# A transformer block in emulated fp32: seven-product steps for the second FFN's first matrix, transposes issued by ScalarE, and a norm spread over one more tile

## The chip, the core and the metric

The kernel runs on one core of a Trainium2 chip. The time is that of the device for one call, in microseconds (us); lower is better. The core's engines work side by side and each takes its instructions in order: PE (TensorE) multiplies, DVE (VectorE) and ACT (ScalarE) work on elements, POOL (GpSimd) does little here, and SP (SyncE) issues transfers. DMA engines carry the transfers out.

## The reference, cut to what matters

One block for a sequence of 256 rows and a width of 2048: two feed-forward networks (FFN) around a mixer of attention and convolution. Each part works on a normed and modulated x, and adds to x.

```python
def modulate(h, shift, scale):
    return h * (1 + scale[:, None, :]) + shift[:, None, :]

def swiglu(h, w_gu, w_down):
    gu = jnp.einsum('bsd,df->bsf', h, w_gu)        # 2048 -> 2 * 5632
    g, u = jnp.split(gu, 2, axis=-1)
    return jnp.einsum('bsf,fd->bsd', jax.nn.silu(g) * u, w_down)

    ada = jnp.einsum('bd,de->be', c_act, w_ada[l]) + b_ada[l]
    sh1, sc1, g1, shm, scm, gm, sh2, sc2, g2 = jnp.split(ada, N_MOD, axis=-1)
    h = modulate(rms_norm(x, ffn1_norm[l]), sh1, sc1)
    x = x + FFN_RESIDUAL_WEIGHT * g1[:, None, :] * swiglu(h, ffn1_w_gu[l], ffn1_w_down[l])
    ...                                             # the mixer, in the same form
    h = modulate(rms_norm(x, ffn2_norm[l]), sh2, sc2)
    x = x + FFN_RESIDUAL_WEIGHT * g2[:, None, :] * swiglu(h, ffn2_w_gu[l], ffn2_w_down[l])
```

All weights are fp32 and are read once from DRAM.

## The kernel before

**Products.** An fp32 product is made of three products of a shorter kind (fp32r): both factors are split into a high and a low part, and high x high, high x low and low x high are summed in a PSUM bank (`mm3`, L329, L333, L334). ACT makes the high part of a weight tile (a cast, L305), DVE the low part (a subtraction, L307). A weight arrives as a `raw` tile of 128 x 2048 (1 MB, four buffers), which `w_tile` splits into two `whi` and two `wlo` tiles of 128 x 1024 (four buffers each).

**An FFN.** The 2 x 5632 gate and up columns are cut into 22 chunks of 256 + 256 columns, and the 2048 rows that are summed over into four K blocks of 512 (`pc` 0 to 3). The 256 rows of x are two tiles of 128 (`t`). A chunk and a K block make one step: four column blocks of 128 rows of K, two row tiles, three products, 24 matmuls of 128 x 512. First, K block 0 of all chunks is done and copied to SBUF (`stage_a`, L666), since the norm of the later K blocks is not there yet; then the chunks follow one by one with K blocks 1 to 3. `finish` adds the kept part (L830), applies silu (L831) and multiplies (L832). The result has to be turned for the down projection: in the second FFN, ACT rearranges it to 16-bit planes (L836), SP issues a DMA transpose (L842), ACT joins the planes again (L845), and ACT and DVE split the turned tile (L350, L351).

**Down.** `down_strassen` takes the 2048 output columns in two halves. For 7 of 22 chunks (`SEVEN`) the step of 2 x 2 blocks is done in seven block products instead of eight (a form of Strassen's), at the price of sums of weight blocks on DVE (`split`, L512, L513, and L547 to L550).

**The norm.** `Norm.piece` scales four column blocks of x; one tile later (`after_tiles(1, ...)`, a list that each tile of products counts down in `tick`) `complete` transposes them on PE (L394), modulates them on DVE (L449) and ACT (L452), and splits them (L453, L454). The modulation is computed on the way: `ada` reads 142 pieces of 1 MB of `w_ada` and multiplies them with c on DVE (L193), spread over the program by `ada_share`.

**The order.** The code is a sequence of calls; a scheduler that knows the tiles' buffers and dependences puts the instructions of each engine in an order at build time. Each engine then runs its own list, with semaphores between them. All transfers are issued by SP.

## Time and profile before

| | before |
|---|---|
| median of 3 runs | 1826.58 us (1826.22 to 1826.65) |
| profiled execution | 1831.11 us, span 1829.3 us |
| PE, DVE, ACT busy | 1802.8, 1519.9, 1008.3 us |
| DMA | 501.68 MB, mean 274 GB/s |

A span goes from the first to the last instruction of the profiled execution. Rows of the profile name the line of the kernel, the engine, the operation, and what is written from what (`wlo<-raw,whi`), by the names in the program; a group has its count, the busy time in us, the mean of one in ns, and the idle time before its instructions with what ended it.

### The profile page before, as it was taken

What the parts mean: (1) busy time and instruction counts of PE and PEld (TensorE: products, weight loads), DVE (VectorE), ACT (ScalarE), POOL (GpSimd) and SP (SyncE); (2) the same over time, 40 slices, a digit from 0 to 9 for tenths busy, and PEclk for the clock granted to TensorE, in tenths of its full rate; (3) what the DMA queues carried; (4) which work ended last, traced back from release to release, by engine and by line L of the source; (5) the groups of instructions that cost most, each with busy time, mean ns of one, the idle gap of its engine ahead of it and who ended that gap; (6) DMA issues with size and microseconds to landing.
All of it is one profiled execution on the core that took longest, in us unless ns stands there. A gap on an engine that the chain in (4) does not pass through costs nothing.

```text
span 1829.3 us, 21896 instructions
## 1 busy us (share of the span) xinstructions
PE 1802.8 (99%) x8117; PEld 1484.0 (81%) x8117; DVE 1519.9 (83%) x2018; ACT 1008.3 (55%) x1521; POOL 28.3 (2%) x29
## 2 busy tenths in 40 slices
PE   7999999999999999999999999999999999999998
PEld 5788888888888887788888787888888888878887
DVE  6889869999898787898999778878887765699877
ACT  6553444444444344566798655664665565555453
POOL 0000000000000000000110100000000000000000
PEclk9999999999999999999999999999999999999999
DMA  9987978888889998775444466889899877655552
GB/s 373 349 307 297 347 274 310 327 314 337 337 330 350 355 343 327 290 261 206 176 147 162 160 254 241 328 337 346 262 313 298 302 242 222 203 207 210 204 214 109
DMA packets 95962, 501.68 MB, mean 274 GB/s; under 512 B 31424, under 2 KB 31856, under 8 KB 38384
## 3 DMA queue, kind: packets, MB, share of 16 engines
q1 hardware_dynamic: 95856, 500.30, 74.4%
q8 instruction: 63, 1.03, 0.2%
q14 instruction: 43, 0.35, 0.1%
HBM read 492.37 MB, written 2.12 MB: 270 GB/s over the span
## 4 chain that ended last, share of the span: by engine, by line
PE 85%; DVE 6%; DMA 4%; ACT 3%; issue 2%; POOL 0%; POOLq 0%; DVEq 0%; SPq 0%; ACTq 0%
PE acc L333 27%; PE acc L334 27%; PE acc L329 27%; DVE wlo L307 2%; DMA tmp<-tmp 1%; DMA xall<-in_x_dram 1%; PE tp L333 1%; PE tp L334 1%; DMA raw<-in_w_ada_dram 1%; PE tp L329 1%; ACT whi L305 1%; PE acc L1137 1%; DVE raw L193 1%; DVE wlo L513 1%; DVE blk L1029 1%
## 5 line engine op out<-in xcount | busy, mean ns | idle before, releaser
L333 PE MATMUL acc<-wlo,blk 128*128 128x512 f32 x2340 | 913.7, 390 | 6.9 <-DVE wlo L307 6.9
L329 PE MATMUL acc<-whi,blk 128*128 128x512 f32 x2343 | 911.4, 392 | 1.9 <-ACT blk L403 1.4
L334 PE MATMUL acc<-whi,blk 128*128 128x512 f32 x2340 | 912.3, 390 | 0.1
L305 ACT CAST whi<-raw 128x1024 fp32r<-128x1024 f32 (+1 forms) x581 | 597.3, 1044 | 473.3 <-PE acc L334 333.9
L307 DVE TENSOR_TENSOR wlo<-raw,whi 128x1024 fp32r<-128x1024 f32 (+1 forms) x581 | 691.1, 1210 | 177.7 <-ACT whi L305 176.6
L333 PEld LDWEIGHTS acc<-wlo,blk 128*128 128x128 f32 x2340 | 439.6, 188 | 103.1 <-DVE wlo L307 12.9
L329 PEld LDWEIGHTS acc<-whi,blk 128*128 128x128 f32 x2343 | 439.9, 188 | 93.4 <-ACT blk L403 1.8
L334 PEld LDWEIGHTS acc<-whi,blk 128*128 128x128 f32 x2340 | 439.3, 188 | 91.9 <-DVE blk L405 0.7
L193 DVE CUSTOM_DVE_ANT_0 raw<-raw,c_bc 128x2048 f32<-128x2048 f32 x142 | 324.2, 2285 | 10.3 <-DMA raw<-in_w_ada_dram 10.3
L512 ACT CAST whi<-raw 128x1024 fp32r<-128x1024 f32 (+1 forms) x56 | 53.0, 947 | 68.4 <-PE tp L334 31.9
L513 DVE TENSOR_TENSOR wlo<-raw,whi 128x1024 fp32r<-128x1024 f32 (+1 forms) x56 | 60.8, 1087 | 19.1 <-ACT whi L512 18.9
L666 ACT COPY blk<-acc 128x512 f32<-128x512 f32 x72 | 42.0, 590 | 62.9 <-PE acc L334 60.2
L1029 DVE SCALAR_TENSOR_TENSOR blk<-blk,cst,blk 128x245 f32<-128x245 f32 (+21 forms) x176 | 70.4, 457 | 0.6 <-ACT blk L1027 0.5
L845 ACT COPY tmp<-tmp 128x1024 uint16<-128x1024 uint16 x22 | 29.8, 1355 | 51.2 <-DMA tmp<-tmp 51.2
L830 DVE TENSOR_TENSOR blk<-acc,blk 128x512 f32<-128x512 f32 x88 | 56.6, 682 | 0.0
L831 ACT ACTIVATE blk<-blk 128x256 f32<-128x256 f32 x88 | 33.7, 413 | 20.5 <-DVE blk L830 20.4
L329 PE MATMUL acc<-blk,blk 128*128 128x512 f32 x104 | 41.3, 401 | 1.2 <-ACT blk L321 1.2
L333 PE MATMUL acc<-blk,blk 128*128 128x512 f32 x100 | 39.1, 391 | 0.6 <-DVE blk L307 0.6
L334 PE MATMUL acc<-blk,blk 128*128 128x512 f32 x100 | 39.0, 392 | 0.0
L351 DVE TENSOR_TENSOR blk<-tmp,blk 128x512 fp32r<-128x512 f32 x22 | 15.1, 688 | 26.0 <-ACT blk L350 26.0
L832 DVE TENSOR_TENSOR blk<-blk 128x256 f32<-128x256 f32 x88 | 33.8, 417 | 0.4 <-ACT blk L831 0.4
L836 ACT COPY tmp<-blk 128x1024 uint16<-128x1024 uint16 x22 | 22.9, 1042 | 14.2 <-DVE blk L832 14.1
(227 smaller groups left out, 1058.7 us busy)
## 6 DMA issues: line engine op xcount, KB each, us to landing
raw<-in_w_gu_dram SPq DMA_DIRECT2D x161, 1024.0 KB, 6.0
raw<-in_w_ada_dram SPq DMA_DIRECT2D x142, 1024.0 KB, 6.3
raw<-in_w_dn_dram SPq DMA_DIRECT2D x88, 1024.0 KB, 5.4
raw<-in_w_in_dram SPq DMA_DIRECT2D x40, 1024.0 KB, 4.8
raw<-in_w_out_dram SPq DMA_DIRECT2D x16, 1024.0 KB, 4.8
raw<-in_w_gu_dram SPq DMA_DIRECT2D x8, 768.0 KB, 6.5
blk<-in_w_gu_dram SPq DMA_DIRECT2D x10, 512.0 KB, 13.5
blk<-gate_line SPq DMA_DIRECT2D x6, 512.0 KB, 4.8
```

Of the source, the lines that this page charges most:

```text
L193: nc.vector.tensor_tensor_reduce(out=raw, in0=raw, in1=c_bc, scale=1.0, scalar=0.0, op0=ALU.mult, op1=ALU.add, accum_out=ada_cols[g][:, j ...
L305: nc.scalar.copy(out=hi[:, :m, :], in_=rw)
L307: nc.vector.tensor_sub(out=lo[:, :m, :], in0=rw, in1=hi[:, :m, :].bitcast(F32))
L329: nc.tensor.matmul(acc, ah, wh, start=start, stop=False)
L333: nc.tensor.matmul(acc, ah, wl, start=False, stop=False)
L334: return nc.tensor.matmul(acc, al, wh, start=False, stop=stop)
L512: nc.scalar.copy(out=hi[:, :n, :], in_=src)
L513: nc.vector.tensor_sub(out=lo[:, :n, :], in0=src, in1=hi[:, :n, :].bitcast(F32))
L666: last_part[0] = nc.scalar.copy(out=parts[c][:, t, :], in_=accs[t])
L830: nc.vector.tensor_add(out=p[:, t, :], in0=accs[t], in1=p[:, t, :])
L832: nc.vector.tensor_mul(out=p[:, t, 256:], in0=p[:, t, :256], in1=p[:, t, 256:])
L1029: nc.vector.scalar_tensor_tensor(out=y[:, d:], in0=u, scalar=w, in1=y[:, d:], op0=ALU.mult, op1=ALU.add)
```

## The change

It has several parts.

1. **Second FFN, gate and up.** Two neighbouring chunks make a pair; seven pairs (`PAIRS_2`) do K block 3 with seven block products (`pair_first`), 42 matmuls instead of 48. The sums of x blocks are made once (`pair_sums`, as `sums_of` does for down), those of weights for each pair: four subtractions of 128 x 1024 on DVE, seven splits instead of four. ACT copies a bank (`kept`, L710) before PE adds the next product to the same bank; the copies are used in place of the parts that K block 0 left before. The pair's other K blocks follow in the same banks.
2. **Its order.** `AHEAD_2` names how many K blocks of chunks 0 to 13 come first, `REST_2` the order of the chunks and pairs after that.
3. **x** lies in four tiles of the `blk` pool instead of one of its own, loaded in halves; in the second FFN it is written to DRAM (`spill`) and read again at chunk 16 of the down projection (`fetch`).
4. **Transposes by DMA** are issued by ACT (L959), and the join (L970) is called two tiles later.
5. **The norm** takes a tile for its transposes (`turn`, L414) and completes one tile later (modulation L476 and L479, cast L480, low part L481). From the mixer on, modulation is formed for four columns at once and the bias is added for eight.
6. `KEPT` (the sums that the second half of down takes over from the first) is 7 instead of 6, and `ada` is spread a little differently.

```diff
-KEPT = 6
+KEPT = 7
 CROSSBAR = {0: False, 96: True}
+AHEAD_2 = (1,) * 6 + (2,) * 4 + (3,) * 4
+REST_2 = (6, 10, 14, 7, 0, 11, 16, 8, 2, 12, 18, 9, 4, 20, 13)
+PAIRS_2 = (0, 2, 4, 14, 16, 18, 20)
+ROOM_2 = (2, 2, 2, 1, 0, 0, 0)
...
-            after_tiles(1, lambda: self.complete(kb, t))
+            after_tiles(1, lambda: self.turn(kb, t))
+        def turn(self, kb, t):
+            if (kb, t) in self.open:
+                self.turned[kb, t] = self.transposed(self.open.pop((kb, t)))
+                after_tiles(1, lambda: self.complete(kb, t))
 
         def complete(self, kb, t):
-            if (kb, t) not in self.open:
+            if (kb, t) in self.open:
+                self.turned[kb, t] = self.transposed(self.open.pop((kb, t)))
+            if (kb, t) not in self.turned:
                 return
-            tp, hf = self.transposed(self.open.pop((kb, t)))
+            tp, hf = self.turned.pop((kb, t))
...
+    def pair_first(w_gu, c, pc, act, sums, banks, room):
+        raws = []
+        for n in range(2):
+            raw = rawp.tile([P, 4, 512], F32, tag="raw", name=nm("raw"))
+            w_dma[0] = nc.sync.dma_start(out=raw, in_=w_gu[c + n, pc].rearrange("p (k n) -> p k n", k=4))
+            raws += [raw[:, 0:2, :], raw[:, 2:4, :]]
+        b11, b21, b12, b22 = raws
+        c11, c21, c12, c22 = banks
+        def split(src, own=False):
+            hi = blk([P, 2, 512], F32R) if own else whp.tile([P, 2, 512], F32R, tag="whi", name=nm("whi"))
+            lo = blk([P, 2, 512], F32R) if own else wlp.tile([P, 2, 512], F32R, tag="wlo", name=nm("wlo"))
+            nc.scalar.copy(out=hi, in_=src)
+            nc.vector.tensor_sub(out=lo, in0=src, in1=hi.bitcast(F32))
+            return hi, lo
+        def times(acc, a, w, start=False):
+            for j in range(2):
+                mm3(acc, a(j), (w[0][:, j, :], w[1][:, j, :]), start and j == 0, j == 1, more=not start)
+        def kept(acc):
+            u = tmp([P, 512])
+            nc.scalar.copy(out=u, in_=acc)
+            return u
+        k0 = 4 * pc
+        t2 = blk([P, 2, 512])
+        nc.vector.tensor_sub(out=b12, in0=b12, in1=b11)
+        nc.vector.tensor_sub(out=t2, in0=b22, in1=b12)
+        times(c22, lambda j: act(k0 + j, 0), split(b11, room > 0), True)
+        u11 = kept(c22)
+        nc.vector.tensor_sub(out=b11, in0=t2, in1=b11)
+        times(c12, lambda j: sums[j][0], split(b12, room > 1), True)
+        u22 = kept(c12)
+        times(c22, lambda j: sums[j][1], split(t2))
+        u12 = kept(c22)
+        nc.vector.tensor_sub(out=t2, in0=b21, in1=t2)
+        times(c21, lambda j: act(k0 + 2 + j, 1), split(t2), True)
+        times(c11, lambda j: act(k0 + 2 + j, 0), split(b21), True)
+        times(c22, lambda j: sums[j][2], split(b11))
+        u21 = kept(c22)
+        times(c12, lambda j: sums[j][3], split(b22))
+        tick()
+        tick()
+        return [u11, u21, u12, u22]
+    xd = dramp.tile([P, NT, 2, 1024], F32, name="x_kept")
+    def spill(i):
+        if i < 2 * NT:
+            nc.sync.dma_start(out=xd[:, i // 2, i % 2], in_=xb[i // 2][i % 2])
+    def fetch(h):
+        for t in range(NT):
+            xb[t][h] = blk([P, 1024])
+            nc.sync.dma_start(out=xb[t][h], in_=xd[:, t, h])
...
-            for c in range(3, NCH):
-                w = w_tile(w_gu[c, 0])
-                stage_a(c, w, [acc_tile() for _ in range(NT)], (0, 1))
-                ada_a_share(4)
-                pieces()
+            for c, n in enumerate(AHEAD_2):
+                start_of[c] = n
+                if c < 3:
+                    continue
+                accs = [acc_tile() for _ in range(NT)]
+                for pc in range(n):
+                    ada_until(base + 8 * pc + 8)
+                    pieces(last_part[0] if ada_next[0] >= base + 32 else None)
+                    w = w_tile(w_gu[c, pc])
+                    mm_tile(accs, w, act, 4 * pc, pc == 0, pc == n - 1)
+                    ada_a_share(4)
+                    pieces(last_part[0] if ada_next[0] >= base + 32 else None)
+                parts[c] = blk([P, NT, 512])
+                for t in range(NT):
+                    last_part[0] = nc.scalar.copy(out=parts[c][:, t, :], in_=accs[t])
+                spill(c - 6 if c >= 6 else 9)
...
-        def finish(c, accs):
-            p = parts[c]
+        def finish(c, accs, us=None):
+            p = parts[c] or blk([P, NT, 512])
+            m = tmp([P, NT, 256]) if CROSSBAR[base] else p[:, :, 256:]
             for t in range(NT):
-                nc.vector.tensor_add(out=p[:, t, :], in0=accs[t], in1=p[:, t, :])
-                nc.scalar.activation(out=p[:, t, :256], in_=p[:, t, :256], func=AF.Silu)
-                nc.vector.tensor_mul(out=p[:, t, 256:], in0=p[:, t, :256], in1=p[:, t, 256:])
-
+                gu = p[:, t, :] if us or parts[c] else accs[t]
+                if us or parts[c]:
+                    nc.vector.tensor_add(out=gu, in0=accs[t], in1=us[t] if us else gu)
+                nc.scalar.activation(out=p[:, t, :256], in_=gu[:, :256], func=AF.Silu)
+                nc.vector.tensor_mul(out=m[:, t, :], in0=p[:, t, :256], in1=gu[:, 256:])
             if CROSSBAR[base]:
-                planes = tmp([P, 2, NT, 256], U16)
-                nc.scalar.copy(out=planes, in_=p[:, :, 256:].bitcast(U16).rearrange("p t (f b) -> p b t f", b=2))
+                planes, turned = p[:, 0, :].bitcast(U16), p[:, 1, :].bitcast(U16)
+                nc.scalar.copy(out=planes.rearrange("p (b f) -> p b f", b=2),
+                               in_=m.rearrange("p t f -> p (t f)").bitcast(U16).rearrange("p (f b) -> p b f", b=2))
 
             def rest():
+                if CROSSBAR[base]:
+                    nc.scalar.dma_start_transpose(out=turned.rearrange("p (j s) -> p j s", s=P), in_=planes)
+                    after_tiles(2, joined)
+                    return
+                tp = tp_tile((P, 2, S))
+                for t in range(NT):
+                    for i in range(2):
+                        nc.tensor.transpose(tp[:, i, t * P:(t + 1) * P], m[:, t, i * P:(i + 1) * P], ident)
+                halves(tp)
+            def joined():
+                src = p[:, 0, :].rearrange("p (i t s) -> p i t s", i=2, t=NT)
+                nc.scalar.copy(out=src.bitcast(U16).rearrange("p i t (s b) -> p b t i s", b=2),
+                               in_=turned.rearrange("p (b t i s) -> p b t i s", b=2, t=NT, i=2))
+                halves(src.rearrange("p i t s -> p i (t s)"))
+            def halves(src):
                 a = blk([P, 2, 2, S], F32R)
-                if CROSSBAR[base]:
-                    turned = tmp([P, 2, NT, 2, P], U16)
-                    nc.sync.dma_start_transpose(out=turned.rearrange("p b t i s -> p (b t i) s"),
-                                                in_=planes.rearrange("p b t f -> p (b t f)"))
-                    src = tmp([P, 2, NT, P])
-                    nc.scalar.copy(out=src.bitcast(U16).rearrange("p i t (s b) -> p b t i s", b=2), in_=turned)
-                    src = src.rearrange("p i t s -> p i (t s)")
-                else:
-                    src = tp_tile((P, 2, S))
-                    for t in range(NT):
-                        for i in range(2):
-                            nc.tensor.transpose(src[:, i, t * P:(t + 1) * P],
-                                                p[:, t, 256 + i * P:256 + (i + 1) * P], ident)
                 split_from_psum(src, a[:, 0], a[:, 1])
                 aT[c] = a
 
             after_tiles(1, rest)
...
-        groups = [[0, 1, 2]] + [[c] for c in range(3, NCH)]
+        groups = [[0, 1, 2]] + [[c] for c in range(3, NCH)] if base == 0 else [[c] for c in REST_2]
         pend = []
-        for g in groups:
+        pairs = 0
+        for i_g, g in enumerate(groups):
+            if base > 0 and i_g == 1:
+                ada_until(base + 32)
+                pieces(last_part[0])
+                for t in range(NT):
+                    st.complete(3, t)
+                sums = pair_sums(st.hh[3], st.hl[3])
+            if base > 0 and g[0] in PAIRS_2:
+                c = g[0]
+                banks = [acc_tile(), acc_tile()]
+                banks += [tp_tile(), tp_tile()] if pairs % 2 else [acc_tile(), acc_tile()]
+                pairs += 1
+                us = pair_first(w_gu, c, 3, act, sums, banks, ROOM_2[pairs - 1])
+                for pc in range(start_of[c], 3):
+                    for n in range(2):
+                        w = w_tile(w_gu[c + n, pc])
+                        mm_tile(banks[2 * n:2 * n + 2], w, act, 4 * pc, False, pc == 2, more=True)
+                        ada_share(ada_b[0], ada_b[1])
+                        while pend:
+                            finish(*pend.pop(0))
+                        if parts[c] and pc == start_of[c]:
+                            for t in range(NT):
+                                u = parts[c + n][:, t, :]
+                                nc.vector.tensor_add(out=u, in0=us[2 * n + t], in1=u)
+                                us[2 * n + t] = u
+                for n in range(2):
+                    pend.append((c + n, banks[2 * n:2 * n + 2], us[2 * n:2 * n + 2]))
+                continue
...
-    ffn(norm2, w_gu2, w_dn2, 128, (0.78, 128), (0.5, 144), None, [], [[3], [4], [5]], [])
+    ffn(norm2, w_gu2, w_dn2, 128, (0.75, 128), (0.32, 144), None, [], [], [])
```

The scheduler's lists show how this moves the work. On PE, before, at the second tile of the norm's K block 3 in the second FFN (`tp_1940`; `blk_1845` and `blk_1846` are the high and low parts of K block 2, and `blk_1929` the high part of block 3, which is first read 22 matmuls after the transposes):

```order
L334 MATMUL acc_1897_10272<-whi_1926_10427,blk_1846_10029 128x512
L329 MATMUL acc_1898_10273<-whi_1934_10467,blk_1845_10028 128x512 [waits Activation_49]
L329 MATMUL acc_1899_10274<-whi_1934_10467,blk_1845_10028 128x512
L394 MATMUL tp_1940_10515<-cst_87,tmp_1932_10463 128x128 x3
L333 MATMUL acc_1898_10273<-wlo_1935_10469,blk_1845_10028 128x512 [waits DVE_49]
L334 MATMUL acc_1898_10273<-whi_1934_10467,blk_1846_10029 128x512
L333 MATMUL acc_1899_10274<-wlo_1935_10469,blk_1845_10028 128x512
L334 MATMUL acc_1899_10274<-whi_1934_10467,blk_1846_10029 128x512
```

Here products with block 2 follow the transposes. The same place after (`tp_1888` and `tp_1890` are the two tiles, `blk_1876` and `blk_1877` the high and low parts of block 3):

```order
L353 MATMUL acc_1882_10225<-whi_1886_10232,blk_1802_9804 128x512
L414 MATMUL tp_1888_10260<-cst_87,tmp_1878_10217 128x128 x4
L414 MATMUL tp_1890_10266<-cst_87,tmp_1879_10219 128x128 x4
L348 MATMUL acc_1881_10224<-whi_1893_10274,blk_1876_10215 128x512 [waits Activation_49]
L352 MATMUL acc_1881_10224<-wlo_1894_10276,blk_1876_10215 128x512 [waits DVE_49]
L348 MATMUL acc_1904_10343<-whi_1907_10347,blk_1876_10215 128x512
L352 MATMUL acc_1904_10343<-wlo_1908_10349,blk_1876_10215 128x512 [waits DVE_49]
L353 MATMUL acc_1881_10224<-whi_1893_10274,blk_1877_10216 128x512 [waits DVE_49]
L348 MATMUL acc_1882_10225<-whi_1893_10274,blk_1876_10215 128x512 [waits Activation_49]
```

Both tiles' transposes now stand directly ahead of the first product that reads what is made of them.

On ACT, before, a stretch of the second FFN's later chunks (L305 a weight's high part, L831 silu, L836 the planes, L845 the join, L350 the split):

```order
L831 ACTIVATE blk_1721_9444<-blk_1721_9444 128x256 [waits DVE_49] x2
L305 CAST whi_2056_11138<-raw_2055_11136 128x1024 [waits DMAHW0_49,PE_49]
L836 COPY tmp_2046_11093<-blk_1721_9444 128x1024 [waits DVE_49]
L305 CAST whi_2058_11142<-raw_2055_11136 128x1024 [waits PE_49,Activation_49]
L305 CAST whi_2064_11178<-raw_2063_11176 128x1024 [waits DMAHW2_49,PE_49,Activation_49]
L845 COPY tmp_2054_11132<-tmp_2053_11130 128x2x2x2x128 [waits DMAHW4_49]
L350 CAST blk_2052_11129<-tmp_2054_11132 128x512 [waits Activation_49]
L305 CAST whi_2066_11182<-raw_2063_11176 128x1024 [waits DVE_49,PE_49]
L305 CAST whi_2070_11220<-raw_2069_11218 128x1024 [waits DMAHW3_49,DVE_49,PE_49]
L305 CAST whi_2072_11224<-raw_2069_11218 128x1024 [waits DVE_49,PE_49]
```

The join waits there for a transfer that SP issued, among casts of weights. After, in the first pair (L700 high parts of the pair's weights, L710 the kept copies, L959 the transpose's issue, L950 silu, L970 the join):

```order
L700 CAST whi_1925_10423<-blk_1918_10395 128x1024 [waits DVE_49,PE_49]
L710 COPY tmp_1921_10408<-acc_1915_10390 128x512 [waits PE_49]
L959 DMA_TRANSPOSE blk_1742_9485<-blk_1742_9485 128x8x128 [waits Activation_49]
L950 ACTIVATE blk_1815_9872<-blk_1815_9872 128x256 [waits DVE_49]
L710 COPY tmp_1924_10421<-acc_1914_10389 128x512 [waits PE_49]
L970 COPY blk_1742_9485<-blk_1742_9485 128x2x2x2x128 [waits DMAHW0_49]
L710 COPY tmp_1927_10433<-acc_1915_10390 128x512 [waits PE_49]
L700 CAST whi_1928_10436<-blk_1918_10395 128x1024 [waits DVE_49]
L700 CAST whi_1930_10446<-raw_1916_10391 128x1024
L700 CAST whi_1932_10456<-raw_1916_10391 128x1024
L700 CAST whi_1935_10468<-raw_1917_10393 128x1024 [waits Activation_49]
```

The transpose is now issued between two kept copies, and its join stands ahead of the third. On SP before, the transposes stood among the loads of weights:

```order
L294 DMA raw_10792<-in_w_gu_dram 128x2048 [waits DVE_49]
L192 DMA raw_10833<-in_w_ada_dram 128x2048 [waits DMAHW2_49,DVE_49]
L842 DMA_TRANSPOSE tmp_10724<-tmp_10671 128x8x128 [waits PE_49]
L294 DMA raw_10839<-in_w_gu_dram 128x2048 [waits DMAHW3_49,DVE_49,Activation_49]
L842 DMA_TRANSPOSE tmp_10731<-tmp_10679 128x8x128
L294 DMA raw_10881<-in_w_gu_dram 128x2048 [waits DVE_49]
L842 DMA_TRANSPOSE tmp_10738<-tmp_10687 128x8x128 [waits DMAHW4_49,DMAHW0_49,Activation_49]
```

After, SP has no transposes in its list.

More of the change, by code (lines that the diff above doesn't have):

```diff
@@ L121, in block_kernel, with xs @@
     pos_i = const.tile([P, NT], I32, name="pos_i")
[L122 to L123 removed]
+    xb = [[blk([P, 1024]) for _ in range(2)] for _ in range(NT)]
+    def xs(n, t):
+        return xb[t][n // 2][:, n % 2 * 512:n % 2 * 512 + 512]
     first_cols = _COLS["nm"][0]
@@ L127, in load_x @@
     def load_x(t):
-        return nc.sync.dma_start(out=xall[:, t, :], in_=x_in[t * P:(t + 1) * P, :])
+        for h in range(2):
+            ld = nc.sync.dma_start(out=xb[t][h], in_=x_in[t * P:(t + 1) * P, h * 1024:(h + 1) * 1024])
+        return ld
     load_x(0)
@@ L228, in modulation @@
     def modulation(base, k, norm):
-        if (base, k) not in mods:
+        if (base, k) not in mods and base > 0:
+            ada_until(base + 2 * k // 8 * 8 + 8)
+            a = ada_cols[(base + 2 * k) // 8]
+            k0 = k // 4 * 4
+            G = scales[:, base // 3 + k0:base // 3 + k0 + 4]
+            nc.vector.scalar_tensor_tensor(out=G, in0=a[:, 0:8:2], scalar=1.0, in1=col(norm)[:, k0:k0 + 4],
+                                           op0=ALU.add, op1=ALU.mult)
+            for i in range(4):
+                mods[base, k0 + i] = (G[:, i:i + 1], a[:, 2 * i + 1:2 * i + 2])
+        elif (base, k) not in mods:
             j = base + 2 * k
```

89 lines of the change are left out of this document (55 added, 34 removed).

## The prediction

> **What bounds the kernel now.** I read the page from the top first: busy time, the clock, the chain that ended last.
>
> ```profile
> span 1829.3 us, 21896 instructions
> PE 1802.8 (99%) x8117; PEld 1484.0 (81%) x8117; DVE 1519.9 (83%) x2018; ACT 1008.3 (55%) x1521; POOL 28.3 (2%) x29
> PEclk9999999999999999999999999999999999999999
> PE 85%; DVE 6%; DMA 4%; ACT 3%; issue 2%; POOL 0%; POOLq 0%; DVEq 0%; SPq 0%; ACTq 0%
> ```
>
> TensorE (PE) is busy for 99% of the span at a clock that is never lowered, and 85% of the chain is its work. So a product that is left out is time gained, as long as PE does not wait in its place. A busy PE need not be PE at its peak, so I take the price of one product from the timeline of PE in a stretch without gaps: the first and the last of 28 128x512 matmuls in a row.
>
> ```profile
> 1539.73 0.39 PE L333 MATMUL acc<-wlo,blk 128*128 128x512 f32 x1
> ...
> 1545.85 0.39 PE L333 MATMUL acc<-wlo,blk 128*128 128x512 f32 x1
> ```
>
> Starts lie (1545.85 - 1539.73) / 27 = 0.2267 us apart; the 0.39 in the second column is one matmul's length, of which most lies beside the next one. Then the busy time by stretches, PE, PEld, DVE, ACT, POOL, clock, DMA share, GB/s from left to right:
>
> ```profile
> 300.00:400.00 100.00, 100.00 (x458) 82.73 (x457) 94.41 (x117) 46.97 (x63) 0.00 (x0) 1.00 0.88 327
> 900.00:1000.00 100.00, 99.36 (x534) 84.03 (x533) 97.00 (x217) 92.05 (x296) 11.89 (x9) 1.00 0.43 155
> 1200.00:1600.00 400.00, 398.85 (x1759) 328.82 (x1758) 296.63 (x343) 235.45 (x279) 0.00 (x0) 1.00 0.82 279
> 1600.00:1700.00 100.00, 99.41 (x437) 81.21 (x436) 92.04 (x125) 57.30 (x64) 0.00 (x0) 1.00 0.56 210
> ```
>
> The third row is most of the second FFN's gate and up products, where the change sits: PE lost 1.15 us in 400, VectorE (DVE) is 74% busy, ScalarE (ACT) 59%. The first row shows that 94% on DVE alone need not stop PE.
>
> **The products.** Seven pairs each do their K block 3 in 42 matmuls instead of 48. The order of PE counts 7638 matmuls of 128x512 before and 7596 after, 42 fewer: 42 x 0.2267 = **-9.5 us**. Nothing hides on PE, so that is the whole possible gain of the pairs.
>
> **What DVE and ACT get for it.** Prices, mean ns of one in the fifth field, from the groups by line:
>
> ```profile
> L307 DVE TENSOR_TENSOR wlo<-raw,whi 128x1024 fp32r<-128x1024 f32 x230 | 275.0, 1220 | 87.4 <-ACT whi L305 87.2
> L305 ACT CAST whi<-raw 128x1024 fp32r<-128x1024 f32 x230 | 235.9, 1049 | 83.4 <-PE acc L334 48.5 <-DMA raw<-in_w_gu_dram 11.5 <-PE tp L334 10.9
> L666 ACT COPY blk<-acc 128x512 f32<-128x512 f32 x44 | 25.7, 589 | 41.0 <-PE acc L334 39.4
> L831 ACT ACTIVATE blk<-blk 128x256 f32<-128x256 f32 x88 | 33.7, 413 | 20.5 <-DVE blk L830 20.4
> L842 SPq DMA_TRANSPOSE tmp<-tmp x22: 1237/1239/2462, 1295.3 to 1596.8; - x22
> DMA to landing us min/median/max: 3.3/4.5/8.8
> ACT tmp L845 <- DMA tmp<-tmp: 51.2, 22, 4.3
> ```
>
> By the order, DVE gets 49 more operations of 128x1024 (28 sums of weights, 21 low halves): 49 x 1.22 = 59.8 us. ACT gets 21 casts (22.0 us), 12 more 128x512 copies (28 kept products, 16 part copies fewer: 7.1 us) and 22 transpose issues, whose price on ACT no row shows; on SP one is 1.24 us, so 27.3 us (the ends: 0, if ACT only hands it on, and 2.46 each). All of it falls on about the stretch of the third row. DVE there becomes 296.6 + 59.8 = 356 of 400 (89%); ACT, with the 51.2 us in which it waits for transposes, 235.5 + 51.2 + 22.0 + 7.1 + 27.3 = 343 of 400 (86%). Neither becomes the bound over the stretch; but inside one pair step DVE has 11 such operations, 13.4 us, for PE's 42 x 0.2267 = 9.5, so the step draws 3.9 us from the lead. The lead is four weight buffers of each kind, and between two pair steps lie some 200 matmuls (46 us).
>
> What such a step costs PE is shown by the down projection, which runs seven-product steps already: 14 of them, seven in each half of the output. On PE's timeline of 1600 to 1630 us the matmuls that started late:
>
> ```profile
> 1611.94 0.39 PE L329 MATMUL acc<-whi,blk 128*128 128x512 f32 x1
> 1612.64 0.50 PE L333 MATMUL tp<-wlo,in_c_bc 128*128 128x512 f32 x1 [0.31 <-DVE wlo L513]
> 1612.97 0.39 PE L334 MATMUL tp<-whi,in_c_bc 128*128 128x512 f32 x1
> ...
> 1622.32 0.39 PE L334 MATMUL tp<-whi,in_c_bc 128*128 128x512 f32 x1
> 1622.77 0.50 PE L329 MATMUL tp<-whi,in_c_bc 128*128 128x512 f32 x1
> 1623.11 0.40 PE L329 MATMUL acc<-whi,blk 128*128 128x512 f32 x1
> 1623.71 0.50 PE L329 MATMUL acc<-whi,blk 128*128 128x512 f32 x1 [0.21 <-ACT whi L305]
> ```
>
> Each start less 0.2267 after the one before it: 0.47 + 0.10 at 1612, 0.22 + 0.11 + 0.37 at 1623, 1.3 us in two steps, 0.65 each; the steps after them lose nothing until the end of the kernel. So a pair costs between 0 and 0.65 us by this row. The pairs differ from these steps: they wait for ACT's copies of a bank before they add to it again. I take the middle, 0.33, since the two steps that cost 0.65 stood in the stretch with DVE at 92%, close to 89%, and most others cost nothing: 7 x 0.33 = **+2.3 us** (ends 0 and 4.6; the copies' own danger is the rival below).
>
> **The norm, one tile behind.** A norm piece is transposed on PE, modulated by ACT and DVE, cast, and then multiplied. By the order before, 264 and 370 matmuls (60 and 84 us) lay between the transposes of K blocks 1 and 2 of the second FFN and their first product, 22 (5.0 us) for block 3. In the order after, the last transposes stand 5, 4 and 0 matmuls ahead of the first product: 1.13, 0.91 and 0 us. What the path from transposes to the first high half takes is shown in the mixer, where a piece is finished at once (timeline):
>
> ```profile
> 785.76 1.04 PE L394 MATMUL tp<-cst,tmp 128*128 128x128 f32 x8
> ...
> 787.22 1.16 ACT L452 ACTIVATE tmp<-tp,ada,scales 128x128 f32<-128x128 f32 x3 [1.76 <-DVE tmp L449]
> ...
> 788.27 0.63 ACT L453 CAST blk<-tmp 128x512 fp32r<-128x512 f32 x1
> ...
> 789.89 0.69 DVE L454 TENSOR_TENSOR blk<-tmp,blk 128x512 fp32r<-128x512 f32 x1
> ```
>
> Transposes end at 785.76 + 1.04 = 786.80, the high half at 788.90: 2.10 us. So the three places cost 0.97 + 1.19 + 2.10 = **+4.3 us**. Ends: the low half there ended at 790.58, 3.78 us after the transposes; where PE waits for that, the places cost 2.65 + 2.87 + 3.78 = 9.3. Below: ACT began 0.42 us after the transposes, held by DVE; if it begins at once, 3 x 0.42 less, 3.0. The mixer's second piece keeps 9 products (2.04 us) against 2.10: nothing. FFN1's pieces keep 9.5 us and more: nothing.
>
> **Stalls that leave.** The largest two waits of PE in the stretch stood where the order is now another:
>
> ```profile
> 1320.43 0.39 PE L329 MATMUL acc<-whi,blk 128*128 128x512 f32 x1
> 1321.17 0.50 PE L333 MATMUL acc<-wlo,blk 128*128 128x512 f32 x1 [0.36 <-DVE wlo L307]
> ...
> 1419.42 0.39 PE L329 MATMUL acc<-whi,blk 128*128 128x512 f32 x1
> 1420.60 0.50 PE L333 MATMUL acc<-wlo,blk 128*128 128x512 f32 x1 [0.79 <-DVE wlo L307]
> 1420.94 0.40 PE L334 MATMUL acc<-whi,blk 128*128 128x512 f32 x1
> ```
>
> 0.74 - 0.23 = 0.51 and 1.18 - 0.23 = 0.95, with 0.11 more behind each: **-1.7 us**, or nothing if new ones stand in their place.
>
> **The start.** x comes in two halves per tile, so the squares of the first columns can start before the second half lands. Now ACT's two stand behind the whole load:
>
> ```profile
> 6.55 0.63 ACT L360 ACTIVATE tmp<-xall 128x512 f32<-128x512 f32 x1 [1.50 <-DMA xall<-in_x_dram]
> ...
> 7.64 0.63 ACT L360 ACTIVATE tmp<-xall 128x512 f32<-128x512 f32 x1
> ```
>
> At best the first of them (1.09 us to the second's start) is gone from the path, at worst nothing; I take **-0.6**.
>
> **At nothing.** SP loses 22 issues of 1.24 us and gets 10 of plain transfers: it waits more than it issues. x written out (four of 512 KB) and fetched again adds 4.2 MB, 15 us at the 279 GB/s of the third row, in stretches with a DMA share of 0.82 and, for the fetch, 0.56: idle engines cover both; without that cover, weights would land up to 15 us later in sum. The fetch stands six steps ahead of its use. Joined modulation (one operation for four columns) and bias sums take some 60 DVE operations of under 0.25 us away, which DVE's idle time covers. A seventh kept set of sums saves DVE a rebuild in the second half of down, where PE did not wait for it. Three ada columns moved into the output projection lie beside PE work.
>
> **The sum.** -9.5 + 2.3 + 4.3 - 1.7 - 0.6 = -5.2 us. The profiled execution took 1831.1 us (span 1829.3), 4.5 above the median 1826.6; it would become 1825.9, and the median **1821.4**. Own range of this case 1817.5 to 1822.9, with the terms' ends partly against each other.
>
> **Rivals.**
> - *The turned transposes hold up ACT, and ACT holds up the pair (slower).* ACT works in order. In the first pair it issues a transpose between the copy of the first product and the next, and the join that waits for that transpose stands ahead of the copy u12 and of the casts of the next weights, for all of which PE waits. From the issue to the join ACT has 1.24 + 0.41 (silu) + 0.59 of work; the transpose lands 4.5 us after its issue: 2.3 us idle. Some eight joins stand like that in six of the pairs: 8 x 2.3 = 18 us on ACT; less a lead of about 0.8 each, 12 us on PE, so 1821.4 + 12 = **1833**. It decides where PE has under 2.3 us of other products queued: the copy is waited for directly, so that is likely in pairs 1, 3 and 5. Against it: before, the 22 joins idled ACT for 51.2 us in the third row's stretch and PE lost 1.15 us in all of it. For it: there ACT was 59% busy and ran far ahead, now it is 86% loaded.
> - *Within noise.* The 4.3 stands, the pairs cost their 4.6, and the stalls that left come back elsewhere: -9.5 + 4.3 + 4.6 - 0.6 = -1.2, **1825.4**. For it speaks that DVE is at 89%, and that the stretch of the second row, with 97%, shows 0.64 us of waits in 100.
> - *Nothing waits in the pairs and the norm's path is at its lower end.* -9.5 + 3.0 - 1.7 - 0.6 = -8.8, **1817.8**. The first row speaks for it (94% on DVE, no PE wait); against it the leads of 5, 4 and 0 matmuls, which are in PE's own order.
>
> On the first rival, one row has two readings: transposes landed in 3.3 to 8.8 us while they shared SP's queue with loads of 1 MB. The Trainium skill, DMA: Bandwidth & Descriptors, section Queues, rings and completion order, says that each DMA engine takes turns between the queue rows at packet granularity; SP and ACT own one each. By that rule a transpose on ACT's queue would not stand behind the loads and land near the 3.3 of the row, the idle time per join falls from 2.3 to 1.1, and that rival to about 1824. The same page, section Issuing engines are not separate DMA queues, says that issuing from several engines saves only issuing time; by that, 4.5 stays, and so does 1833. No run before shows a transpose on ACT's queue.
>
> **Chances.** A difference under 0.2% (3.7 us) can hardly be told from no change here. My case has 0.36, the better one 0.14 (both faster), within noise 0.20, held up 0.30. Faster 0.50, same 0.20, slower 0.30. The range, 8 in 10: from 1815, a little below the better case, to 1837, a little above the held-up one.
>
> **What would show it.** Right: PE's count of 128x512 at 42 fewer; at each of the three norm places a PE wait of 1 to 2 us on ACT's cast; in the pair steps waits under 0.7 us on DVE's low halves. The held-up case would show as PE waits on ACT, L700 or L710, of 1 to 3 us in several pairs, with ACT's wait for the join just before. The prediction is wrong on the high side if DVE's 3.9 us per pair are not made up before the next pair, which would show as DVE over 97% from pair to pair, and on the low side if the three norm waits are missing.

## The result

The changed kernel takes 1918.1 us (median of 4 runs, 1910.1 to 1926.8) against 1826.45 of the kernel before: 1.0503 times as long, 95% interval 1.0462 to 1.0543. The forecast was 1821.4, with a range up to 1837. The page of the profiled execution, the longest of the four (span 1925.0 us):

```profile
span 1925.0 us, 21896 instructions
PE 1825.1 (95%) x8075; PEld 1489.6 (77%) x8075; DVE 1573.8 (82%) x2013; ACT 1036.3 (54%) x1555; POOL 27.4 (1%) x29
PEclk9999999999999999999999999999989889899999
q1 hardware_dynamic: 74064, 498.72, 70.9%
q10 hardware_dynamic: 23232, 5.77, 2.6%
```

PE has its 42 matmuls fewer (x8117 before, x8075 here), but is busy 22 us longer and stands still for 100 of 1925 us, before for 26.5. The clock, at nine tenths or more in every slice before, is lowered in four slices between 1396 and 1684 us. A second DMA queue, q10, has appeared: it is ACT's, with 22 x 1056 packets for the 22 transposes. The stretches, first of the kernel before, then of this one (PE, PEld, DVE, ACT, POOL, clock, DMA share, GB/s); the second row of each runs to about the first product of the down projection:

```profile
1102.00:1285.00 183.00, 182.71 (x818) 150.49 (x817) 151.00 (x183) 103.92 (x143) 0.56 (x1) 1.00 0.84 320
1285.00:1591.90 306.90, 305.75 (x1347) 251.97 (x1346) 221.70 (x260) 186.34 (x217) 0.00 (x0) 1.00 0.80 264
```

```profile
1102.00:1285.00 183.00, 174.13 (x766) 141.58 (x765) 148.85 (x173) 100.08 (x134) 0.56 (x1) 0.99 0.77 292
1285.00:1683.00 398.00, 335.05 (x1352) 265.40 (x1351) 275.00 (x304) 213.00 (x256) 0.00 (x0) 0.91 0.73 208
```

The stage with the pairs and the transposes takes 398 us where it took 307, at a clock of 0.91, and no engine is the bound in it: PE is busy for 84%, DVE 69%, ACT 54%, DMA 73%. It is a stage of waits. What waited for what, from 1102 us on (total us, times, longest):

```profile
PE acc L348 <- ACT whi L324: 32.0, 6, 10.2
PE tp L348 <- ACT tmp L710: 8.0, 2, 7.8
PE acc L348 <- ACT tmp L710: 7.5, 4, 4.4
PE acc L348 <- ACT whi L700: 6.7, 5, 2.3
ACT blk L970 <- DMA blk<-blk: 91.5, 18, 17.0
ACT whi L324 <- issue: 17.0, 6, 12.1
```

PE waits for ACT, and ACT stands at the join (L970), where it waits for a DMA transpose. The longest of PE's waits, from the timelines of ACT and PE:

```profile
1521.00 1.25 ACTq L959 DMA_TRANSPOSE blk<-blk  x1
1522.34 2.11 ACT L324 CAST whi<-raw 128x1024 fp32r<-128x1024 f32 x2 [1.38 <-issue]
1541.44 1.33 ACT L970 COPY blk<-blk 128x1024 uint16<-128x1024 uint16 x1 [16.99 <-DMA blk<-blk]
...
1543.32 1.04 ACT L324 CAST whi<-raw 128x1024 fp32r<-128x1024 f32 x1
```

```profile
1533.85 0.39 PE L353 MATMUL acc<-whi,blk 128*128 128x512 f32 x1
1544.41 0.79 PE L348 MATMUL acc<-whi,blk 128*128 128x512 f32 x1 [10.18 <-ACT whi L324]
1545.67 0.79 PE L352 MATMUL acc<-wlo,blk 128*128 128x512 f32 x1 [0.47 <-DVE wlo L326]
...
1546.69 0.63 PE L348 MATMUL acc<-whi,blk 128*128 128x512 f32 x1
1547.12 0.63 PE L352 MATMUL acc<-wlo,blk 128*128 128x512 f32 x1
```

The transpose issued at 1521 is awaited until 1541.4. PE lives off weight tiles that were split before until 1534, then waits 10.2 us, and after that its matmuls start 0.43 us apart and not 0.227, until 1551. In the stage 72 starts lie 0.42 to 0.43 apart: 72 x 0.2 = 14 us for the clock alone. The transposes themselves, issue durations in ns (min, median, max) and the time from issue to landing in us:

```profile
L959 ACTq DMA_TRANSPOSE blk<-blk x22: 1247/1253/11587, 1275.7 to 1688.6; - x22
DMA to landing us min/median/max: 3.1/7.0/21.3
```

Before, on SP's queue, landing was 3.3, 4.5 and 8.8. What is in flight beside a transpose decides. Two windows of the DMA view: 1505 to 1506.7 us, with the queue of loads idle, and 1523 to 1540.5 us, with two loads of 1 MB under way (packets, MB, share of 16 engines; then issue to landing):

```profile
q10 hardware_dynamic: 1056, 0.26, 81.2%
blk<-blk ACTq DMA_TRANSPOSE x1, 3.1
```

```profile
q1 hardware_dynamic: 361, 2.58, 86.6%
q10 hardware_dynamic: 1043, 0.26, 11.4%
raw<-in_w_ada_dram SPq DMA_DIRECT2D x1, 1024.0 KB, 19.0
raw<-in_w_gu_dram SPq DMA_DIRECT2D x1, 1024.0 KB, 19.1
```

In the second the loads too take 19 us each, where 6 is usual, and all queues together move 163 GB/s. Both sides are slowed.

### The profile page after: what moved, and what is told of

Same layout as the page of the kernel before. It is cut to its first block, busy times and chain, and to the rows that moved or that the text cites. A ratio compares the mean times of both kernels' runs of the same rounds, so it can differ in the third digit from the quotient of the medians.

```text
span 1925.0 us, 21896 instructions
## 1 busy us (share of the span) xinstructions
PE 1825.1 (95%) x8075; PEld 1489.6 (77%) x8075; DVE 1573.8 (82%) x2013; ACT 1036.3 (54%) x1555; POOL 27.4 (1%) x29
## 5 line engine op out<-in xcount | busy, mean ns | idle before, releaser
L348 PE MATMUL acc<-whi,blk 128*128 128x512 f32 x2249 | 884.6, 396 | 53.3 <-ACT whi L324 32.0
L352 PE MATMUL acc<-wlo,blk 128*128 128x512 f32 x2246 | 885.0, 394 | 16.7 <-DVE wlo L326 12.7
L353 PE MATMUL acc<-whi,blk 128*128 128x512 f32 x2246 | 881.6, 393 | 0.1
L324 ACT CAST whi<-raw 128x1024 fp32r<-128x1024 f32 x553 | 570.7, 1045 | 529.4 <-PE acc L353 406.7
L326 DVE TENSOR_TENSOR wlo<-raw,whi 128x1024 fp32r<-128x1024 f32 x553 | 658.3, 1211 | 169.0 <-ACT whi L324 167.7
L348 PEld LDWEIGHTS acc<-whi,blk 128*128 128x128 f32 x2249 | 427.5, 190 | 149.5 <-ACT whi L324 34.5
L352 PEld LDWEIGHTS acc<-wlo,blk 128*128 128x128 f32 x2246 | 426.0, 190 | 114.4 <-DVE wlo L326 20.5
L539 ACT CAST whi<-raw 128x1024 fp32r<-128x1024 f32 (+1 forms) x56 | 52.8, 946 | 66.6 <-PE tp L353 31.9
L970 ACT COPY blk<-blk 128x1024 uint16<-128x1024 uint16 x22 | 29.6, 1346 | 91.5 <-DMA blk<-blk 91.5
L540 DVE TENSOR_TENSOR wlo<-raw,whi 128x1024 fp32r<-128x1024 f32 (+1 forms) x56 | 60.8, 1088 | 20.3 <-ACT whi L539 20.0
L1180 DVE SCALAR_TENSOR_TENSOR blk<-blk,cst,blk 128x247 f32<-128x247 f32 (+21 forms) x176 | 70.5, 460 | 0.0
L348 PE MATMUL tp<-whi,blk 128*128 128x512 f32 x149 | 60.0, 403 | 10.8 <-ACT tmp L710 8.0
L352 PE MATMUL tp<-wlo,blk 128*128 128x512 f32 x149 | 59.4, 398 | 2.4 <-DVE wlo L326 2.3
L371 DVE TENSOR_TENSOR blk<-blk,blk 128x512 fp32r<-128x512 f32 x22 | 15.1, 687 | 56.0 <-ACT blk L370 56.0
L353 PE MATMUL tp<-whi,blk 128*128 128x512 f32 x149 | 58.9, 396 | 0.0
L348 PE MATMUL acc<-blk,blk 128*128 128x512 f32 x112 | 44.4, 396 | 0.3 <-ACT blk L340 0.3
L348 PEld LDWEIGHTS tp<-whi,blk 128*128 128x128 f32 x149 | 28.6, 192 | 19.1 <-ACT tmp L710 8.9
L352 PE MATMUL acc<-blk,blk 128*128 128x512 f32 x108 | 42.4, 393 | 0.7 <-DVE blk L326 0.4
```

The lines of the kernel that those rows point to most:

```text
L324: nc.scalar.copy(out=hi[:, :m, :], in_=rw)
L326: nc.vector.tensor_sub(out=lo[:, :m, :], in0=rw, in1=hi[:, :m, :].bitcast(F32))
L348: nc.tensor.matmul(acc, ah, wh, start=start, stop=False, skip_group_check=more)
L352: nc.tensor.matmul(acc, ah, wl, start=False, stop=False, skip_group_check=more)
L353: return nc.tensor.matmul(acc, al, wh, start=False, stop=stop, skip_group_check=more)
L371: nc.vector.tensor_sub(out=lo, in0=tp, in1=hi.bitcast(F32))
```

## Experiments

**SP issues again.** The one line that moved the issue is undone; pairs, order, norm and everything else stay.

```diff
-                    nc.scalar.dma_start_transpose(out=turned...
+                    nc.sync.dma_start_transpose(out=turned...
```

> The changed kernel with one line undone: SP issues the DMA transposes again. Theory A (transposes on ACT's queue take turns, packet by packet, with the 1 MB loads on SP's queue, so they land late, and ACT stands at the join): the transposes land in 3 to 9 us as before, no join holds ACT for more than 6 us, no PE wait of over 3 us stays in the second FFN, the clock stays at 1.0, and the time is 1815 to 1840 us. Rival B (the pair steps themselves overload ACT and DVE, or their kept copies stop PE): the time stays above 1880 us, with PE waits of 4 us and more in the pairs.

1844.5 us, 1.0094 (1.0079 to 1.0109) of before. 73.6 of the 91.6 us are gone with one line, PE's waits of 4 us and more are gone (the longest left is 2.1), and the joins wait 6.3 us in all. It lies a little above the range that the theory gave, and the clock was still lowered once in the stage: 18 us stay.

```profile
DMA to landing us min/median/max: 3.0/3.4/7.0
1285.00:1601.80 316.80, 310.70 (x1349) 253.16 (x1349) 273.11 (x302) 214.27 (x256) 0.00 (x0) 0.99 0.76 260
```

**The kernel before, ACT issues.**

```diff
-                    nc.sync.dma_start_transpose(out=turned.rearrange("p b t i s -> p (b t i) s"),
+                    nc.scalar.dma_start_transpose(out=turned.rearrange("p b t i s -> p (b t i) s"),
```

> The kernel before with that one line of the change alone: ACT issues the DMA transposes, nothing else is new. Theory A: they land in up to 15 to 20 us where a load is in flight, ACT waits at the joins for far more than the 51 us of before, and the time rises to 1850 to 1920 us. Rival B (only the pair steps are hurt by the transposes' issue, or the pairs alone cost the time): within 10 us of the kernel before.

1877.8 us, 1.0249 (1.0208 to 1.0291). The line alone costs 50 us without any pair. ACT's wait at the joins grows from 51.2 to 87.6 us, and PE's waits for ACT's casts, 0.2 us in this stage before, to 28.0:

```profile
DMA to landing us min/median/max: 3.1/5.1/13.8
ACT tmp L845 <- DMA tmp<-tmp: 87.6, 21, 11.5
PE acc L329 <- ACT whi L305: 28.0, 7, 7.7
```

**Neither ACT nor its queue.** SP issues the transposes, and GpSimd the weight loads of that stage, so that the two kinds lie on two queues again, but ACT issues nothing.

```diff
-            w_dma[0] = nc.sync.dma_start(out=raw[:, :n, :], in_=src[:, k0:k0 + n, :])
+            w_dma[0] = (nc.gpsimd if pool_loads[0] else nc.sync).dma_start(out=raw[:, :n, :], in_=src[:, k0:k0 + n, :])
...
-            w_dma[0] = nc.sync.dma_start(out=raw, in_=w_gu[c + n, pc]...
+            w_dma[0] = nc.gpsimd.dma_start(out=raw, in_=w_gu[c + n, pc]...
```

> The changed kernel with transposes issued by SP and the second FFN's weight loads of the stage after the norm (w_tile and pairs) issued by GpSimd, on its own queue; the w_ada pieces stay on SP's queue, ahead of and behind the transposes. ACT issues no transfer. Theory Q (a transpose and a 1 MB load that are in flight on two queues at once slow each other down, whoever issues): transposes land in 8 us and more in several cases, loads later than 6 us, and the time is 1870 to 1920 us. Rival I (it was the issue by ACT that was slow): transposes land in 3 to 7 us as with SP alone, and the time is 1840 to 1855 us.

1895.1 us, 1.0371 (1.0355 to 1.0387): 51 above SP alone. Transposes land in up to 18.3 us. In its window of 1495 to 1509 us SP's queue (a transpose and the end of a w_ada load) and GpSimd's queue share the engines again:

```profile
DMA to landing us min/median/max: 3.0/4.5/18.3
q1 hardware_dynamic: 1132, 0.88, 52.8%
q0 software_dynamic: 267, 1.92, 51.5%
raw<-in_w_ada_dram SPq DMA_DIRECT2D x1, 1024.0 KB, 15.3
```

So transposes land late although ACT issues none: it takes transposes and loads in flight on two queues at once. GpSimd's own way of issuing is not the reason: counted over this trace, its 28 loads of the stage with no transpose in flight landed in 5.0 to 8.4 us (median 5.1), the 27 beside one in up to 17.5. With SP issuing both (the first run), w_gu loads beside a transpose landed in 4.8 to 8.0 us. That ACT's slow issues add something of their own is not excluded.

**Smaller packets.** ACT issues; loads are cut into four transfers of 512 columns (2 KB a packet); the loads of the pairs and the w_ada pieces from 100 on are cut in the same way.

```diff
-            w_dma[0] = nc.sync.dma_start(out=raw[:, :n, :], in_=src[:, k0:k0 + n, :])
+            for k in range(n):
+                w_dma[0] = nc.sync.dma_start(out=raw[:, k, :], in_=src[:, k0 + k, :])
```

> The changed kernel, ACT still issuing the transposes, but each 1 MB load of a w_tile, of a pair and of the later w_ada pieces is cut into four transfers of 512 columns, so that a packet of a load is 2 KB and not 8 KB. Theory A: a transpose has 1024 packets, 64 for each of 16 DMA engines, and each takes turns with one packet of a load; with packets of a quarter of the size the longest landing falls from 21 us to 5 to 10 us, and the time to 1835 to 1880 us. Rival C (it is the issue by ACT, or a switch between queues whatever the packets' size, that is slow): longest landing of 15 us and more, time above 1895 us.

1918.2 us, 1.0499 (1.0483 to 1.0515): no gain in the whole, and outside the theory's range. The longest landing fell, from 21.3 to 14.1, less than expected, and the median did not:

```profile
L963 ACTq DMA_TRANSPOSE blk<-blk x22: 1247/1300/4270, 1292.4 to 1682.8; - x22
DMA to landing us min/median/max: 3.1/7.7/14.1
```

PE still had waits of 8.3 and 11.3 us. But the unchanged time is the sum of a loss and a gain. The cut loads cost time before any transpose by DMA is in flight: PE transposes the norm's K block 3 at 1274.9 us (L417), with whole loads at 1259.8 (L414). The down projection's first sums of x blocks are cast at 1698.2 us (L532), with whole loads at 1704.9 (L529). So the stretch with the transposes is 22 us shorter, some 15 at least, since the execution with whole loads was 9 us above its median and this one 2. With SP issue the same stretch is 81 us shorter: packets of 2 KB win back about a quarter.

**What the packets show.** The packets' own records in these traces say more than the landings. An 8 KB packet of a load usually takes 0.31 us. In the changed kernel eight transposes land in 12.4 us or more, and during each of them 12 to 17 such packets stay open for 3 to 7.8 us; during the other 14, which land in 9.5 us or less, none does. The same is seen in the kernel before with ACT issue (38 packets), with GpSimd's loads (50, on both queues) and with GpSimd's joins (87, two runs below). It is not seen once among the more than 9000 load packets of the stage in each run where transposes share SP's queue with all loads, nor in the run without transposes by DMA. With packets of 2 KB none stays open for 3 us either. So the engines do not simply take turns, packet by packet; the window above, with 361 packets beside 1043, is not one for one either. What holds the large packets is open, and so is why the run with small ones keeps most of its loss.

**The turn on PE.** No DMA transposes at all: the second FFN's result is turned by PE, as in the first (`CROSSBAR = {0: False, 96: False}`); the rest of the change stays. Without the transposes 1822 to 1850 us was expected, and above 1880 if they were not the loss.

1867.8 us, 1.0221 (1.0205 to 1.0236): between the two, and 23 us above SP issue. The 88 transposes keep PE busy for 13.4 us, and PE waits 6.2 us for low parts of the turned tiles (`PE tp L348 <- DVE blk L371`). It confirms that 50 of the 92 us leave with the DMA transposes from ACT, and that the rest of the change is no gain with this turn either.

**Join and split on GpSimd.** ACT issues the transposes, but no longer stands at the join.

```diff
-                nc.scalar.copy(out=src.bitcast(U16)...
+                nc.gpsimd.tensor_copy(out=src.bitcast(U16)...
...
-                halves(src.rearrange("p i t s -> p i (t s)"))
...
+                nc.gpsimd.tensor_copy(out=a[:, 0], in_=src)
+                nc.gpsimd.tensor_sub(out=a[:, 1], in0=src, in1=a[:, 0].bitcast(F32))
...
```

> The changed kernel, ACT still issuing the transposes, but the join and the split of the turned tile done by GpSimd (POOL), which is nearly idle, so that nothing on ACT or DVE stands in wait for a transpose. Theory A1 (late transposes cost time because ACT stands at the join in front of casts that PE needs): the PE waits of 4 to 10 us go but for those of slow issues on ACT (17 us in all), and the time falls from 1918 to 1845 to 1870 us. Rival A2 (transposes and loads on two queues slow each other down, and late loads are what PE waits for): still above 1890 us, with ACT waiting for loads of weights.

1902.7 us, 1.041 (1.0387 to 1.0433): only 15 of the 92 us go, as the rival expected, so ACT's standing was not all of it. With the joins away, ACT's waits show another part, late weight loads and slow issues:

```profile
ACT whi L324 <- DMA raw<-in_w_gu_dram: 52.2, 14, 10.0
ACT whi L324 <- issue: 19.2, 3, 16.5
DMA to landing us min/median/max: 3.1/6.2/23.9
L701 DVE TENSOR_TENSOR wlo<-blk,whi 128x1024 fp32r<-128x1024 f32 x14 | 20.7, 1479 | 2.4 <-ACT whi L700 2.4
```

The last row is a disturbance by the experiment itself: beside GpSimd's work DVE's subtractions take 1479 ns on average where they took 1220. With SP issue the same move costs 18 us (next two runs), so ACT's standing may be worth some 15 + 18 = 33 us here; that is an estimate, since the two need not add up:

**SP issue, GpSimd joins, early w_ada.** The kernel with SP issue, with the edit above and `(1.5, 128)` in place of `(0.75, 128)` in the call of the second `ffn`.

> A version to beat both: SP issues the transposes, GpSimd joins and splits, and the second FFN's w_ada pieces come twice as fast ahead. It takes 22 joins of 1.35 us and 22 casts of 0.62 us off ACT and 22 subtractions of 0.69 us off DVE, of which the pair steps have too little. If the pairs' waits (7 to 8 us) come from ACT and DVE being behind, half of them go: 1828 to 1834 us. If they come from the kept copies alone: as with SP issue and early w_ada, about 1836.

1881.8 us, 1.0304 (1.0287 to 1.0322), where 1828 to 1836 was expected: slower than SP issue alone and than the kernel before.

**Early w_ada alone.** SP issue.

```diff
-    ffn(norm2, w_gu2, w_dn2, 128, (0.75, 128), (0.32, 144), None, [], [], [])
+    ffn(norm2, w_gu2, w_dn2, 128, (1.5, 128), (0.32, 144), None, [], [], [])
```

> The changed kernel with transposes issued by SP, and in the second FFN the pieces of w_ada taken twice as fast ahead (1.5 instead of 0.75 for each tile of products), so that the modulation of K blocks 1 to 3 is there sooner: by the order the norm's transposes then stand 96, 264 and 336 matmuls ahead of their first product instead of 5, 4 and 0. Theory D (the short leads come from the late modulation, and cost the 1.9 + 1.9 + 2.2 + 2.8 us of PE waits seen around them): these waits go and the time falls by 7 to 9 us against the kernel with SP issue alone, 1844.5 to about 1836. Rival E (DVE is short of time there, and the sooner pieces of w_ada only move the waits): within 3 us of 1844.5.

1863.5 us, 1.0199 (1.0183 to 1.0214): 19 slower than with the late ones, and outside both expectations. PE now waits 15.4 us for DVE's low halves (`PE acc L352 <- DVE wlo L326`), and 415 matmuls are recorded between 1102 and 1225 us where SP issue alone had 533. So the late modulation is not what the 18 us hang on; that the sooner multiplications stand in DVE's way is likely from this wait, but not shown. GpSimd's joins cost another 18 (the run above).

**No pairs.** SP issue; the seven pairs are done as plain chunks.

```diff
-REST_2 = (6, 10, 14, 7, 0, 11, 16, 8, 2, 12, 18, 9, 4, 20, 13)
-PAIRS_2 = (0, 2, 4, 14, 16, 18, 20)
+REST_2 = (6, 10, 14, 15, 7, 0, 1, 11, 16, 17, 8, 2, 3, 12, 18, 19, 9, 4, 5, 20, 21, 13)
+PAIRS_2 = ()
```

> The changed kernel with transposes issued by SP and no pairs: each of the seven pairs is done as two plain chunks, 48 matmuls for K block 3, 7638 in all. Everything else (ahead stage, order of the chunks, norm) stays. If the pairs give back in waits what they save (7 to 8 us of PE waits in the pair steps against 9.5 us): 1841 to 1848 us. If they are worth their 9.5 us: 1851 to 1856. If they cost more than they save: below 1841.

1836.2 us, 1.0046 (1.0031 to 1.0061): 8.3 faster than with the pairs. With their order of chunks, they cost about 18 us to save 9.5. Without them PE is never idle in the stage:

```profile
1285.00:1594.90 309.90, 309.90 (x1369) 256.68 (x1368) 207.44 (x227) 180.69 (x208) 0.00 (x0) 1.00 0.78 258
```

**DVE's load beside the pairs.** SP issue; most of the multiplication of the last 16 w_ada pieces is left out. DVE's busy time between 1285 and 1590 us falls from 262 to 237 us.

```diff
-        nc.vector.tensor_tensor_reduce(out=raw, in0=raw, in1=c_bc, scale=1.0, ...
+        w_ = 64 if j >= 128 else D
+        nc.vector.tensor_tensor_reduce(out=raw[:, :w_], in0=raw[:, :w_], in1=c_bc[:, :w_], scale=1.0, ...
```

> The changed kernel with transposes issued by SP; of the last 16 pieces of w_ada only 64 of 2048 columns are multiplied (the gates of the last residual come out of a part of the sums), the loads stay. DVE gets 16 x 2.2 = 35 us back in the stage with the pairs. Theory P1 (the pairs' 11 us of PE waits come from DVE, which has 13.4 us of work for 9.5 us of PE in a pair step): half of them or more go, 1835 to 1840 us. Rival P2 (they come from ACT, which has casts, kept copies, joins and splits in a row): within 2 us of 1844.5.

1845.7 us, 1.0098 (1.0084 to 1.0112): no difference. DVE's multiplications of w_ada are not what the pairs wait for; the pairs' own sums and low halves on DVE were not touched.

**ACT's joins in the pairs.** SP issue; the join copies 16 columns, the split reads a constant.

```diff
-                nc.scalar.copy(out=src.bitcast(U16)...
+                nc.scalar.copy(out=p[:, 0, :8].bitcast(U16), in_=turned[:, :16])
-                halves(src.rearrange("p i t s -> p i (t s)"))
+                halves(c_bc[:, :512].rearrange("p (i s) -> p i s", i=2))
```

> The changed kernel with transposes issued by SP; the join is a copy of 16 columns that only waits for the transpose, and the split reads a constant tile instead of the joined one (the down projection then multiplies a constant). ACT gets 22 x 1.2 = 26 us back in the stage with the pairs, DVE nothing. Theory P2 (ACT's work in a row is what the pairs wait for): half of the 11 us go, 1835 to 1840 us. Rival P1 (DVE): within 2 us of 1844.5.

1846.1 us, 1.0103 (1.009 to 1.0117). In the profiled executions the first wait that both kernels have in the down projection (0.56 us, `PE acc L348 <- ACT whi L324`) stands at 1617.2 us instead of 1620.5, so ACT's joins are worth some 3.3 us up to there; a wait of 3.5 us for the down projection's first sum of x blocks (`PE acc L348 <- ACT in_c_bc L529`), which the edit brought, took them back. By time the run lies where the rival put it, but that added wait makes it no test; by PE's waits for the pairs' high halves (5.2 us with SP issue, 2.6 here) ACT is part of it, not most.

**x in halves.** The kernel before, x loaded in two transfers for each tile of rows.

> The kernel before with x loaded in halves of 512 KB, as in the change, and nothing else. The changed kernels reach the second FFN 1.7 us sooner than before. If that is the halved load at the start: 0.5 to 1.7 us faster than before. If it comes from the norm or the bias sums: no difference.

1828.4 us, 1.0005 (0.9996 to 1.0014): no difference.

## Why the prediction was wrong

**The step that failed is the price of a transpose on ACT's queue.** The sum of -5.2 us has no term for it. Only the rival that was given 0.30 prices it: landing from the row of SP's queue, 4.5 us, and eight joins at 12 us in all. The chain of that rival was right (ACT at the join, PE behind it), but the price was off by a factor of six: the move of the issue costs 73.6 us in this kernel and 50 in the kernel before. The place was right in part: PE's largest waits stood at the casts of plain steps (L324, 32.0 us), not at those of the seven-product steps and their copies (L700 and L710, 22.2 together). And the loads were slowed as well, which no rival had. The range had no end for it, because the uncertain price was bounded by one queue's rows (3.3 to 8.8), none of which shows two queues in flight; 21.3 was measured.

The rule that was weighed there was read in the wrong direction. The Trainium skill, DMA: Bandwidth & Descriptors, section Queues, rings and completion order, says that the DMA engines take turns between queue rows at packet granularity; I made of it that a transpose would no longer stand behind loads and land near 3.3. The runs show that sharing is worse than standing in line: with ACT's queue the landing was 7.0 us at the median and 21.3 at most, with SP's 3.4 and 7.0 in the same kernel, and the loads finished late too. Turns alone do not explain that: single load packets stayed open for up to 7.8 us, where 0.31 is usual. The other reading, by which the 4.5 us would stay, missed as well.

**The clock** was left out of every price. A wait was costed at its own length; in this stage of the changed kernel the waits of 1 us and more were followed by a lowered clock, 14 us in sum. The Trainium skill, TensorE: Matmul & The Clock Gate, section Part 1: The HAM clock gate (the "warmup" mystery), says that about 3.4 us of idle time halve the clock; the distance of 0.43 us between starts after the wait of 10.2 us agrees. With SP issue the same distance followed two waits of 0.99 and 0.76 us:

```profile
1375.01 0.50 PE L348 MATMUL acc<-whi,blk 128*128 128x512 f32 x1 [0.99 <-ACT whi L700]
1376.27 0.50 PE L352 MATMUL acc<-wlo,blk 128*128 128x512 f32 x1 [0.76 <-DVE wlo L701]
...
1377.40 0.63 PE L353 MATMUL acc<-whi,blk 128*128 128x512 f32 x1
1377.83 1.05 PE L348 MATMUL acc<-whi,blk 128*128 128x512 f32 x2
```

There no wait was near 3.4 us, so the measurement decides: short waits in a row were enough here. They are not always: two waits of 1.13 and 0.77 us at 1469 us of the same execution were followed by the full clock. What decides between the two is open.

**The products** came out as said: 42 fewer. **The pairs' own cost** was mis-sized: 2.3 us by the middle of 0 and 0.65 each, about 18 by the two kernels with SP issue (9.5 saved, 8.3 lost), 2.5 us for each pair. The seven-product steps of down were the wrong measure. The w_ada part of DVE's load is not it (run without the late multiplications). In one of the pairs that lose most, ACT's join and its copy of a bank stand ahead of a cast that PE waits for, and a wait of 0.77 us for DVE's low half follows: the timeline of the kernel with SP issue, 1466 to 1470 us.

```profile
1466.60 1.36 ACT L970 COPY blk<-blk 128x1024 uint16<-128x1024 uint16 x1
1467.82 0.57 ACT L710 COPY tmp<-acc 128x512 f32<-128x512 f32 x1
1468.29 1.05 ACT L700 CAST whi<-blk 128x1024 fp32r<-128x1024 f32 x1
1469.39 0.49 PE L348 MATMUL acc<-whi,blk 128*128 128x512 f32 x1 [1.13 <-ACT whi L700]
```

That joins are a part is suggested by the run without them (3.3 us up to the down projection); what the rest hangs on is open. More buffers for split weights were not tried.

**The norm's three places** lost time where the prediction said, and about as much: 4.3 us predicted, 5.5 found. In the changed kernel:

```profile
1148.35 0.50 PE L352 MATMUL acc<-wlo,blk 128*128 128x512 f32 x1 [1.69 <-DVE wlo L326]
1200.25 0.50 PE L352 MATMUL acc<-wlo,blk 128*128 128x512 f32 x1 [1.70 <-DVE wlo L326]
1262.95 0.50 PE L348 MATMUL acc<-whi,blk 128*128 128x512 f32 x1 [2.14 <-ACT blk L480]
```

Only the third is the path that was measured in the mixer (2.10); that the first two are near in size is luck. There PE waited for a weight's low half, which stood behind the norm's modulation in DVE's order. **The stalls that leave** did leave: without pairs PE is busy for 309.90 of 309.90 us. **The start**: x in halves gives nothing. With SP issue PE's first transposes for the second FFN's norm stand at 1099.7 us, 1.7 sooner than in the profiled execution of the kernel before; but with x in halves alone they stand at 1100.1 with no gain in time, so most of that may be a difference between executions.

In sum, by medians, over the kernel before: 9 us for the new order, the norm and the smaller parts (SP issue without pairs), 8 for the pairs, 74 for the issue by ACT.

## What to carry over

A transfer that is moved to another queue is a new transfer: rows of the old queue need not bound its landing, as here, where 1056 packets met a queue full of 8 KB ones. Where a wait ends last on an in-order engine, price what is queued behind it and the clock that follows, not the wait alone. When the whole time of a run stays the same, look at its stages: a loss in one can hide a gain in another. Undoing one line of a composite change told more here than any sum: of the parts, the one that looked cheapest carried four fifths of the loss.
